# Which engine adds SBUF tiles: GpSimd's share kept for one stretch of a decoder block

## Chip, cores and metric

The kernel runs on one core of one Trainium2 chip, in one launch. Its time is device time in microseconds (us), and lower is better. A core has a matrix engine (TensorE, PE; its weight loads are PEld), VectorE (DVE), ScalarE (ACT), GpSimd (POOL), and a queue (SP) that issues the transfers here. Each engine works off its own queue in order; semaphores tie the queues together. SBUF is the on-chip working memory, and matmuls write to PSUM, which POOL does not read in this kernel.

## What is computed

One decoder block for 1024 tokens of width 1024: a Mamba-2 (SSD) branch and a gated linear attention (GLA) branch from one projection `n @ w_in`, merged by sigmoid gates, then cross-attention to 256 memory tokens, then a SwiGLU FFN of width 2816, with RMSNorm ahead of each and at the end. Cut to its core:

```python
def hybrid_mixer(n, ...):
    z, xBC, dt_raw, q, k, v, r, a1, g_ssd, g_gla = jnp.split(n @ w_in, idx, axis=-1)
    y_ssd = ssd_mixer(z, xBC, dt_raw, ...)
    y_gla = gla_mixer(q, k, v, r, a1, ...)
    merged = sigmoid(g_ssd) * (y_ssd @ w_up_ssd) + sigmoid(g_gla) * (y_gla @ w_up_gla)
    return merged @ w_o

def reference(x, mem, ...):
    h = x
    h = h + hybrid_mixer(rmsnorm(h, norm_mix), ...)
    h = h + mem_cross_attention(rmsnorm(h, norm_xattn), rmsnorm(mem, norm_mem), w_xq, w_xkv, w_xo)
    h = h + swiglu(rmsnorm(h, norm_ffn), w_ffn_in, w_ffn_out)
    return rmsnorm(h, norm_final)
```

## The kernel before

**Products.** A float32 product is made of three products of a narrower float type: each operand x is split into `hi` (a rounded copy, made by ACT) and `lo = x - hi` (a subtraction, on DVE or POOL), and PE adds hi·hi, hi·lo and lo·hi (`split`, line 219). The large projections also use a Strassen-like scheme with seven block products in place of eight. Its sums of blocks are additions of SBUF tiles: those of the activations in `Operands` (lines 226 to 269: operands B11, B21, T1, B22, T2, T3, T4, each with an `h` and an `l` tile), those of the weights in `Unit.left` (lines 290 to 305).

**Units.** A `Unit` makes 256 output columns for all 1024 tokens. It loads `raw` (1 MB of weights), and for each of the seven names it forms the weight block (for T1 the sum `sa` of two blocks; for B22 two subtractions; for T3 one), splits it into `whi` and `wlo`, runs 12 matmuls into an accumulator and evacuates that into `o`. Three accumulators serve a unit: B11, T2, T3 and T4 add up in one of them, T1 and B22 in a second, B21 in a third (line 276), so T4 can't start before T3's result has been read. In PSUM there are four accumulators (`acc`) and four other banks (`bank`).

**Order of the work.** First the memory's k and v and the norm of x, with the operands B formed beside them; then v and two small columns (`v_steps`, line 619, where a weight block is `vraw` and its sum `vsa`); then z (4 units), xBC (6 units, with a convolution), then r, q, k and one gate unit beside the SSD scan; then the other gate units beside the GLA scan; then five dense products (`dense`: w_up_ssd, w_up_gla, w_o, w_xq and, behind the attention, w_xo), with the sums of w_ffn_out's blocks formed beside them (`presum`, line 1190); then the FFN in (22 units, in pairs of gate and up, whose results are multiplied together and stored) and FFN out.

**Who adds.** `DVE` and `POOL` are wrapped in a `Meter` (line 59), which keeps an account `t` of when the engine would be done, by a rate for each. `either` (line 86) gives back the engine that would be done with an addition first; a `slack` of 1 or 2 us in POOL's favour goes with the sums of blocks. `either` is asked by Operands (lines 267 and 268), Unit.left (293, 302), `Stats.take` (465, sums of squares, `ssum`), the split of the memory's weights (561), v_steps (639, 644), the fetch of y's blocks (1175), presum (1200), the merge (1231), the products of gate and up and their block sums (1361 to 1389) and the residual's fold (1498). Other work is put on POOL by name: parts of the convolution and of the SSD scan, small copies, and the power in `rsqrt` (line 207). A plain `DVE` stands for all that reads PSUM, for evacuations above all.

**Queues.** The program is written in an order of its own, and the framework orders each engine's queue when the kernel is built, by priority and by a timeline of its own (line 1606). `ahead()` (line 134) raises the priority of weight blocks and evacuations, and `PRIO` that of the scans' steps. All transfers are issued by SP. As the whole trace shows DVE's and POOL's instructions under line 74 (the Meter's), the groups are told apart by their tiles.

```python
def either(ap, slack=0.0):

    return POOL if POOL.after(ap) - slack < DVE.after(ap) else DVE
```

Of the kernel before, what the change touches and what calls it, by code (L numbers as in the profile page):

```python
# [79 lines left out]
def block_kernel(ctx: ExitStack, tc: tile.TileContext, t: dict, out: bass.AP):  # L80
# [2 lines left out]
    PE, ACT, SP = Tensor(nc.tensor, now), nc.scalar, nc.sync  # L83
    DVE, POOL = Meter(nc.vector, now, 0.06, 1.04e-3), Meter(nc.gpsimd, now, 0.08, 2.25e-3)

    def either(ap, slack=0.0):

        return POOL if POOL.after(ap) - slack < DVE.after(ap) else DVE


    def pool(name, bufs=1, space=None, stack=None, **kw):
# [36 lines left out]
    def bank(dt=F32):  # L128
        return ps.tile([P, 512], dt, name="bank", tag="bank", bufs=4)
# [57 lines left out]
    def col(name, i=0):  # L187
        which, at = gcol[name]
        return cols[:, which, at + i:at + i + 1]
# [199 lines left out]
    def group(units, B, then=(), nxt=None, frm=6, products=7):  # L389


        for u in units:
            u.load()
        then = list(then)
        many = len(units)
        for n, name in enumerate((PAIRED if many > 1 else SPACED)[:products]):
            for x, u in enumerate(units):
                u.step(name, B)
                if many > 1:
                    B.upto((n + 1) * B.kh - (-(x + 1) * B.kh // many))  # L400
                if n == 6 and nxt:
                    nxt.upto((x + 1) * nxt.kh // many)
                if n >= frm and then:
                    then.pop(0).load()
                while len(posts) > lag[0]:
                    settle()
                    if n < 4:
                        break
                yield
        for u in then:  # L410
            u.load()

    def run(main, *rest, prio=0):

        owed = [0.0] * len(rest)
        for _ in main:
            for i, (g, rate) in enumerate(rest):
                owed[i] += rate
                while owed[i] >= 1.0:
                    owed[i] -= 1.0  # L420
                    with tc.high_priority(offset=prio):
                        next(g, None)

    def chain(gs):
        for g in gs:
            yield from g

    def drain(g):
        for _ in g:
            pass  # L430

    def singles(units, B, then=()):

        for u, nxt in zip(units, list(units[1:]) + [None]):
            yield from group([u], B, [nxt] if nxt else then)

    def store_rows(dst, func=None):

        def mk(base):
            def post(i, j, ap):  # L440
                if func is not None:
                    ACT.activation(ap, ap, func)
                SP.dma_start(dst[base + i * P:base + (i + 1) * P, half(j)], ap)
            return post
        return mk

    def w_in_units(c0, n, mk):
        return [Unit(t["w_in"], 0, c0 + 256 * u, post=mk(256 * u)) for u in range(n)]
# [270 lines left out]
    def ssd_prep():  # L719
        bc = lambda r_: r_.unsqueeze(1).to_broadcast([P, NCH, NH])  # L720
        xb, e, l, q = (gp.tile([P, NCH, NH], F32, name=n, tag=n) for n in ("xb", "ex", "ln", "po"))
        m = gp.tile([P, NCH, NH], I32, name="pm", tag="pm")
        add(DVE, xb, dt_t, bc(dtb))
        ACT.activation(e, xb, AF.Abs)
        ACT.activation(e, e, AF.Exp, scale=-1.0)
        ACT.activation(l, e, AF.Ln, bias=1.0)

        DVE.tensor_scalar(q, e, -0.25, 1.0 / 3.0, ALU.mult, ALU.add)
        mul(DVE, q, q, e)
        DVE.tensor_scalar(q, q, -1.0, 0.5, ALU.mult, ALU.add)  # L730
        mul(DVE, q, q, e)
        DVE.tensor_scalar(q, q, -1.0, 1.0, ALU.mult, ALU.add)
        mul(DVE, q, q, e)
        DVE.tensor_scalar(m, e, 0.02, None, ALU.is_lt)
        DVE.copy_predicated(l, m, q)
        DVE.scalar_tensor_tensor(dtv, xb, 0.0, l, ALU.max, ALU.add)
        ea = gp.tile([P, NH], F32, name="ea", tag="ea")
        ACT.activation(ea, alog, AF.Exp)
        a = gp.tile([P, NCH, NH], F32, name="adt", tag="adt")
        DVE.scalar_tensor_tensor(a, dtv, -1.0, bc(ea), ALU.mult, ALU.mult)  # L740
        af = a.rearrange("p c h -> p (c h)")
        yield
        p1, p2, p3 = bank(), bank(), bank()
        PE.matmul(p1[:, :P], triu, af, start=True, stop=True)
        PE.matmul(p2[:, :P], af, triu, start=True, stop=True)
        PE.matmul(p3[:, :P], ones, af, start=True, stop=True)
        ct = gp.tile([P, P], F32, name="ct", tag="ct")
        DVE.tensor_copy(ct, p2[:, :P])
        SP.dma_start(cs_d, ct)
        DVE.tensor_copy(cs, p1[:, :P])  # L750
        sub(DVE, dec, p3[:, :P], cs)
        ACT.activation(dec, dec, AF.Exp)
        ACT.activation(ec, p3[:, :P], AF.Exp)
        yield

    def gla_prep():

        w3, wa2 = (gp.tile([48, 512], d, name=n, tag=n) for n, d in (("w3", F32), ("wa2", F32R)))
        for i in range(3):
            SP.dma_start(w3[16 * i:16 * i + 16], t["gla_w_a2"])  # L760
        ACT.activation(wa2, w3, AF.Copy)
        sub(DVE, wa2[32:48], w3[32:48], wa2[32:48])
        a3 = gp.tile([P, NCH, 48], F32R, name="a3", tag="a3")
        ACT.activation(a3[:, :, 0:16], a1_t, AF.Copy)
        ACT.activation(a3[:, :, 32:48], a1_t, AF.Copy)
        sub(DVE, a3[:, :, 16:32], a1_t, a3[:, :, 0:16])
        idr = gp.tile([P, P], F32R, name="idr", tag="idr")
        ACT.activation(idr, ident, AF.Copy)
        a1T = gp.tile([48, TOK], F32R, name="a1T", tag="a1T")
        keep = gp.tile([P, TOK], F32, name="keep", tag="keep")  # L770
        POOL.memset(keep, 1.0)
        for c in range(NCH):
            POOL.memset(keep[:, c * CH:c * CH + 1], 0.0)
        for j in range(2):
            p = bank()
            for a in range(4):
                PE.matmul(p[:48, a * P:(a + 1) * P], a3[:, 4 * j + a, :], idr, start=True, stop=True)
            DVE.tensor_copy(a1T[:, j * HALF:(j + 1) * HALF], p[:48, :])
        yield
        x_ = gp.tile([P, 4, TOK], F32, name="gx", tag="gx")  # L780
        y_ = gp.tile([P, 4, TOK], F32, name="gy", tag="gy")
        pairs = [slice(h, h + 2) for h in range(0, 4, 2)]
        for h in range(4):
            for j in range(2):
                p = bank()
                PE.matmul(p, wa2[:, h * P:(h + 1) * P], a1T[:, half(j)], start=True, stop=True)
                ACT.activation(x_[:, h, half(j)], p, AF.Identity, bias=col("b_a", h))
            ACT.activation(y_[:, h], x_[:, h], AF.Abs)
            if h % 2:
                yield  # L790
        for h in pairs:
            ACT.activation(y_[:, h], y_[:, h], AF.Exp, scale=-1.0)
            yield
        for h in pairs:
            ACT.activation(y_[:, h], y_[:, h], AF.Ln, bias=1.0)
            yield
        for h in range(4):
            x, y = x_[:, h], y_[:, h]
            DVE.scalar_tensor_tensor(x, x, 0.0, y, ALU.min, ALU.subtract)
            DVE.tensor_tensor_scan(y, keep, x, 0.0, ALU.mult, ALU.add)  # L800
            yv, xv = (v.rearrange("p (c s) -> p c s", s=CH) for v in (y, x))
            bm, bl = yv[:, :, CH // 2 - 1:CH // 2], yv[:, :, CH - 1:CH]
            sub(DVE, xv, yv, bm.to_broadcast([P, NCH, CH]))
            SP.dma_start(bd_d[h * P:(h + 1) * P, :], x)
            POOL.tensor_copy(ebm[:, h], bm.rearrange("p c o -> p (c o)"))
            POOL.tensor_copy(ebl[:, h], bl.rearrange("p c o -> p (c o)"))
            POOL.tensor_copy(ewl[:, h], xv[:, :, CH - 1:CH].rearrange("p c o -> p (c o)"))
            yield
        for e in (ebm, ebl, ewl):
            ACT.activation(e, e, AF.Exp, scale=1.0 / TAU)  # L810
        yield
# [5 lines left out]
    gs = w_in_units(GS0, 4, store_rows(gs_d))  # L817
    gg = w_in_units(GG0, 4, store_rows(gg_d))
    prep = chain([ssd_prep(), gla_prep()])
    run(singles(zu, B, xu[:1]), (prep, .3))  # L820
    drain(prep)
    st2.close()
# [136 lines left out]
    ssd = ssd_steps()  # L959
    run(singles(ru + qk + gs[:1], B, gs[1:2]), (ssd, 16 * 4 / 63), prio=PRIO)  # L960
    drain(ssd)
    st3.close()


# [645 lines left out]
```

## Time and profile before

| | us |
|---|---|
| median of 3 runs | 2016.9 |
| lowest and highest of them | 2014.09 and 2017.74 |
| the profiled execution | 2017.15 |
| its span, from first to last instruction | 2015.4 |

The profile is of that one execution. "Busy" is the time in which an engine has an instruction under way; a group's row gives the line and engine, output tile and inputs, the number of instructions, their busy time and the mean of one, and then the time that the engine sat idle ahead of them and what ended most of it. `<-` in a view of waits reads "waited for". The column PEclk is the share of full speed granted to TensorE. Where a chain of waits is given, it is the work that ended last in that stretch, followed backwards.

The largest groups of POOL's additions over the whole execution, of which the first four are weight sums of units and of presum:

```profile
L74 POOL TENSOR_TENSOR raw<-raw 128x512 f32<-128x512 f32 x68 | 103.6, 1529 | 7.6 <-DVE sa L74 4.8
L74 POOL TENSOR_TENSOR sa<-raw 128x512 f32<-128x512 f32 x56 | 82.6, 1474 | 206.8 <-DMA raw<-in_w_ffn_out_dram 95.2
L74 POOL TENSOR_TENSOR raw<-raw,sa 128x512 f32<-128x512 f32 x48 | 76.8, 1600 | 91.6 <-DVE wlo L74 91.4
L74 POOL TENSOR_TENSOR sa<-sa,raw 128x512 f32<-128x512 f32 x48 | 73.0, 1521 | 172.0 <-DVE wlo L74 172.0
L74 POOL TENSOR_TENSOR o<-o 128x512 f32<-128x512 f32 x39 | 63.4, 1629 | 59.4 <-DVE o L74 34.9
```

### The profile page before, as it was taken

The page shows a single profiled execution, that of the slowest core. Times are in us where ns is not written, and L with a number is a line of the kernel's source. Part 1 is how long each engine was busy: PE and PEld are TensorE (multiplying, and loading weights), DVE is VectorE, ACT ScalarE, POOL GpSimd, SP SyncE. Part 2 cuts the span into 40 slices and gives each one's busy share as a digit, 9 for nine tenths or more (in the row PEclk, how much of TensorE's full clock was granted, in tenths as well). Part 3 has the DMA queues.
Part 4 walks back from the last instruction along what each step waited for, and adds up shares of the span by engine and source line. Part 5 has one row for each costly group of instructions (what it writes and reads, how often), then busy time and mean ns, then how long its engine had stood idle before and what let it go on. Part 6 is the DMA issues. An engine that isn't in the chain of part 4 may idle for free.

```text
span 2015.4 us, 26277 instructions
## 1 busy us (share of the span) xinstructions
PE 1937.9 (96%) x9740; PEld 1617.2 (80%) x9740; DVE 1250.2 (62%) x1763; ACT 897.0 (45%) x1581; POOL 716.9 (36%) x524
## 2 busy tenths in 40 slices
PE   7798899999999999999999999998999999999998
PEld 6797687777777878888878888876888888888887
DVE  5855649879876655633444328566767667674465
ACT  7433844466553555542333226453343343354243
POOL 2612435556554212232134310244454554430002
PEclk9899999999999999999999999999999999999999
DMA  8441332255643755685775520432323323276463
GB/s 286 147 126 62 120 105 106 104 185 184 202 152 115 224 169 157 221 301 193 247 243 188 177 84 22 136 121 89 104 79 110 126 78 105 89 256 228 149 227 127
DMA packets 243365, 309.60 MB, mean 154 GB/s; under 512 B 14986, under 2 KB 162676, under 8 KB 243236
## 3 DMA queue, kind: packets, MB, share of 16 engines
q1 hardware_dynamic: 243236, 307.92, 45.6%
q8 instruction: 76, 1.25, 0.3%
q14 instruction: 53, 0.43, 0.1%
HBM read 211.07 MB, written 96.80 MB: 153 GB/s over the span
## 4 chain that ended last, share of the span: by engine, by line
PE 66%; DVE 8%; DMA 8%; POOL 6%; issue 6%; ACT 4%; SPq 2%; POOLq 0%; ACTq 0%; DVEq 0%
PE acc L52 58%; PE bank L52 7%; POOL raw L74 2%; DVE wlo L74 2%; DVE cv L74 1%; DMA raw<-in_w_in_dram 1%; PE bank L56 1%; POOL sa L74 1%; POOL y L74 1%; ACT whi L220 1%; DVE o L74 1%; DMA sr<-sr_d 1%; DMA vraw<-in_w_in_dram 1%; DMA ga<-yg_d 1%; ACT e L881 1%
## 5 line engine op out<-in xcount | busy, mean ns | idle before, releaser
L52 PE MATMUL acc<-hl,wd 128*128 128x512 f32 x1920 | 439.9, 390 | 1.7 <-DVE hl L74 0.8
L52 PEld LDWEIGHTS acc<-hl,wd 128*128 128x128 f32 x1920 | 360.1, 188 | 77.0 <-DVE hl L74 1.2
L74 DVE TENSOR_TENSOR wlo<-raw,whi 128x512 fp32r<-128x512 f32 x268 | 244.5, 915 | 129.4 <-ACT whi L220 128.7
L220 ACT ACTIVATE whi<-raw 128x512 fp32r<-128x512 f32 x272 | 169.8, 628 | 247.3 <-PE acc L52 194.7
L74 DVE TENSOR_TENSOR o<-acc,o 128x512 f32<-128x512 f32 (+1 forms) x160 | 107.2, 674 | 88.5 <-PE acc L52 85.9
L52 PE MATMUL acc<-fs 128*128 128x512 f32 (+1 forms) x792 | 156.2, 356 | 0.6 <-ACT o L1505 0.5
L74 POOL TENSOR_TENSOR sa<-raw 128x512 f32<-128x512 f32 x56 | 82.6, 1474 | 206.8 <-DMA raw<-in_w_ffn_out_dram 95.2
L52 PEld LDWEIGHTS acc<-fs 128*128 128x128 f32 x792 | 130.7, 189 | 21.6 <-ACT o L1505 0.9
L74 POOL TENSOR_TENSOR sa<-sa,raw 128x512 f32<-128x512 f32 x48 | 73.0, 1521 | 172.0 <-DVE wlo L74 172.0
L220 ACT ACTIVATE fs<-fr 128x1024 fp32r<-128x1024 f32 (+1 forms) x84 | 80.1, 984 | 110.2 <-PE acc L52 43.4
L74 DVE TENSOR_TENSOR fs<-fr,fs 128x1024 fp32r<-128x1024 f32 (+1 forms) x84 | 98.0, 1198 | 39.7 <-ACT fs L220 39.4
L74 POOL TENSOR_TENSOR raw<-raw,sa 128x512 f32<-128x512 f32 x48 | 76.8, 1600 | 91.6 <-DVE wlo L74 91.4
L220 ACT ACTIVATE whi<-sa 128x512 fp32r<-128x512 f32 x96 | 60.4, 629 | 109.2 <-PE acc L52 67.1
L74 POOL TENSOR_TENSOR raw<-raw 128x512 f32<-128x512 f32 x68 | 103.6, 1529 | 7.6 <-DVE sa L74 4.8
L74 DVE TENSOR_TENSOR wlo<-sa,whi 128x512 fp32r<-128x512 f32 x96 | 79.1, 824 | 37.7 <-ACT whi L220 37.5
L74 DVE TENSOR_TENSOR wd<-raw,wd 128x1024 fp32r<-128x1024 f32 x40 | 51.8, 1302 | 65.2 <-ACT wd L220 57.5
L74 DVE TENSOR_TENSOR ga<-acc,ga 128x512 f32<-128x512 f32 x64 | 43.8, 687 | 69.7 <-PE acc L52 56.0
L74 POOL TENSOR_TENSOR o<-o 128x512 f32<-128x512 f32 x39 | 63.4, 1629 | 59.4 <-DVE o L74 34.9
L52 PE MATMUL acc<-B22h,whi 128*128 128x512 f32 x192 | 77.4, 403 | 7.0 <-ACT whi L220 7.0
L52 PE MATMUL acc<-T2h,whi 128*128 128x512 f32 x192 | 77.4, 403 | 3.1 <-ACT whi L220 2.8
L52 PE MATMUL acc<-T2h,wlo 128*128 128x512 f32 x192 | 76.5, 399 | 3.8 <-DVE wlo L74 3.8
L52 PE MATMUL acc<-T1h,whi 128*128 128x512 f32 x192 | 76.2, 397 | 3.8 <-ACT whi L220 3.8
(370 smaller groups left out, 4832.9 us busy)
## 6 DMA issues: line engine op xcount, KB each, us to landing
raw<-in_w_in_dram SPq DMA_DIRECT2D x26, 1024.0 KB, 6.2
raw<-in_w_ffn_in_dram SPq DMA_DIRECT2D x22, 1024.0 KB, 7.6
act_d<-o SPq DMA_DIRECT2D x77, 256.0 KB, 2.0
fr<-act_d SPq DMA_DIRECT2D x35, 512.0 KB, 4.9
raw<-in_w_ffn_out_dram SPq DMA_DIRECT2D x11, 1024.0 KB, 6.9
fr<-down_d SPq DMA_DIRECT2D x20, 512.0 KB, 4.9
down_d<-raw SPq DMA_DIRECT2D x33, 256.0 KB, 2.7
raw<-in_w_xkv_dram SPq DMA_DIRECT2D x8, 1024.0 KB, 10.9
```

Source lines behind the costliest of these rows:

```text
L52: return s.e.matmul(o, x, y, **kw)
L56: return s.e.transpose(o, x, i)
L74: return f(*a, **kw)
L220: ACT.activation(hi, src, AF.Copy)
L881: ACT.activation(s.e[:, h], s.csb[:, h], AF.Relu, bias=cs[:, s.i0 + h:s.i0 + h + 1], scale=-1.0)
```

## The change

`either` gives back POOL only while a flag is set. The flag is set ahead of the first unit behind v (z) and cleared when the SSD scan is done. Outside that stretch every addition that asked `either` goes to DVE, and DVE's account runs on with them. What is put on POOL by name stays there.

```diff
+    shared = [False]
+
     def either(ap, slack=0.0):
 
-        return POOL if POOL.after(ap) - slack < DVE.after(ap) else DVE
+        return POOL if shared[0] and POOL.after(ap) - slack < DVE.after(ap) else DVE
...
     prep = chain([ssd_prep(), gla_prep()])
+    shared[0] = True
     run(singles(zu, B, xu[:1]), (prep, .3))
...
     run(singles(ru + qk + gs[:1], B, gs[1:2]), (ssd, 16 * 4 / 63), prio=PRIO)
     drain(ssd)
+    shared[0] = False
     st3.close()
```

## The prediction

> **What bounds the kernel now.** I began with the profile's page, for its busy shares.
>
> ```profile
> span 2015.4 us, 26277 instructions
> PE 1937.9 (96%) x9740; PEld 1617.2 (80%) x9740; DVE 1250.2 (62%) x1763; ACT 897.0 (45%) x1581; POOL 716.9 (36%) x524
> ```
>
> TensorE (PE) idles 2015.4 - 1937.9 = 77.5 us. Only that, and time in which it ran slowly, can be won. The second view cuts the span into the program's stages (columns: stretch, its length, then busy us and instructions of PE, PEld, DVE, ACT, POOL, then granted clock, DMA share, GB/s).
>
> ```profile
> core 0: us, PE busy (x) PEld busy (x) DVE busy (x) ACT busy (x) POOL busy (x), PEclk, DMA share, GB/s
> 52.00:97.00 45.00, 35.59 (x260) 34.04 (x261) 42.91 (x43) 23.31 (x44) 30.32 (x20) 0.89 0.40 136
> 97.00:175.00 78.00, 77.34 (x635) 77.08 (x636) 40.95 (x77) 25.40 (x45) 11.89 (x14) 1.00 0.34 106
> 175.00:651.00 476.00, 449.46 (x2334) 356.38 (x2333) 359.12 (x515) 255.96 (x471) 236.43 (x177) 0.98 0.42 137
> 651.00:830.00 179.00, 172.48 (x834) 144.74 (x833) 99.98 (x201) 95.24 (x203) 43.30 (x35) 0.99 0.55 172
> 1345.00:1390.00 45.00, 37.20 (x161) 28.06 (x159) 30.40 (x44) 22.74 (x41) 25.42 (x17) 0.96 0.23 76
> 1390.00:1800.00 410.00, 409.82 (x1808) 339.42 (x1809) 292.30 (x336) 166.57 (x281) 203.27 (x133) 1.00 0.33 113
> ```
>
> The stretch from 175 to 651 (the z and xBC units and the SSD scan) keeps the old rule; a third of PE's idle time lies there, out of reach. Elsewhere three stages leave PE idle beside work that the rule places: the start of v (52 to 97, 9.4 us), GLA (651 to 830, 6.5 us) and the start of the FFN (1345 to 1390, 7.8 us). In v's remainder and the FFN's body PE is busy throughout, so nothing can be won there, only lost.
>
> In 52 to 97 VectorE (DVE) is busy 42.91 of 45 us. The view of groups (count, then busy us, mean ns of one, and idle before them) shows that it is slow rather than overloaded; the last row is the same addition later, in 97 to 175, while GpSimd (POOL) does next to nothing.
>
> ```profile
> L74 DVE TENSOR_TENSOR wlo<-raw,whi 128x512 fp32r<-128x512 f32 x10 | 14.5, 1466 | 3.3 <-ACT whi L220 3.3
> L74 DVE TENSOR_TENSOR B22l<-hs,B22h 128x512 fp32r<-128x512 f32 x4 | 5.9, 1497 | 0.0
> L74 DVE TENSOR_TENSOR T1l<-hs,T1h 128x512 fp32r<-128x512 f32 x4 | 4.9, 1228 | 0.0
> L74 DVE TENSOR_TENSOR T2l<-hs,T2h 128x512 fp32r<-128x512 f32 x4 | 4.6, 1200 | 0.0
> L74 DVE TENSOR_TENSOR vraw<-vraw,vsa 128x1056 f32<-128x1056 f32 x1 | 2.3, 2340 | 0.0
> L74 DVE TENSOR_TENSOR wlo<-vraw,whi 128x528 fp32r<-128x528 f32 x2 | 2.0, 1024 | 0.0
> L74 DVE TENSOR_TENSOR T3l<-hs,T3h 128x512 fp32r<-128x512 f32 x4 | 2.5, 688 | 0.0
> ```
>
> The order of time shows why: one kind of addition takes 0.68 or 1.78 us, according to whether POOL is in an addition at that moment.
>
> ```profile
> 58.82 0.68 DVE L74 TENSOR_TENSOR T1l<-hs,T1h 128x512 fp32r<-128x512 f32 x1
> 60.70 1.78 DVE L74 TENSOR_TENSOR T1l<-hs,T1h 128x512 fp32r<-128x512 f32 x1
> 60.24 1.69 POOL L74 TENSOR_TENSOR hs<-hs 128x512 f32<-128x512 f32 x1 [1.89 <-DVE hs L74]
> ```
>
> Where they meet, each takes about 1.7 us, so the pair does two additions in 1.7 us. DVE alone does four in 2.5 us (the row of T3l), so 0.625 us each and 1.25 us for two: both engines together are slower than the faster one alone. The chain of waits and PE's waits say that this stage hangs on DVE:
>
> ```profile
> by line: DVE wlo L74 29.5%; DVE B22l L74 13.0%; DVE T1l L74 10.6%; issue 9.8%; DVE hs L74 8.6%; PE bank L52 7.3%; ACT whi L220 5.4%; DVE vraw L74 5.0%; DVE T2l L74 3.5%; DVE vq L74 2.9%; PE bank L56 1.9%; ACT B22h L220 1.5%; DVE kvs L74 1.3
> PE bank L52 <- DVE wlo L74: 7.0, 4, 3.3
> ```
>
> **The change, part by part.** *Start of v.* POOL gives up these groups:
>
> ```profile
> L74 POOL TENSOR_TENSOR hs<-hs 128x512 f32<-128x512 f32 x14 | 22.0, 1602 | 8.3 <-DVE hs L74 8.3
> L74 POOL TENSOR_TENSOR wlo<-raw,whi 128x512 fp32r<-128x512 f32 x4 | 5.8, 1448 | 12.6 <-ACT whi L220 12.6
> L74 POOL TENSOR_TENSOR vsa<-vsa,vraw 128x1056 f32<-128x1056 f32 x1 | 2.9, 2857 | 3.7 <-DVE wlo L74 3.7
> ```
>
> DVE gains 18 x 0.625 = 11.3 us, and 1.25 us for the one of double width: 12.5 us. It loses the stretching, down to 0.69 us an addition (1.25 for 1056 columns): 10 x 0.78 + 4 x 0.81 + 4 x 0.54 + 4 x 0.51 + 1.1 + 2 x 0.33 = 17.0 us. Net 4.5 us off the engine that sets the end. Bounds: nothing, if PE's next wait is ACT's or a load's; 9.4 us, if every gap closes. I take 4.5, since chain and waits both name DVE. The stage's clock of 0.89 says that some matmuls ran slowly behind the gaps, but what that would give lies behind DVE, so it is not added.
>
> *Start of the FFN.* PE waits here for splits and for the sum of squares; below that, the instructions in front of them in time.
>
> ```profile
> PE acc L52 <- ACT whi L220: 3.1, 4, 1.3
> PE bank L52 <- DVE ssum L74: 2.2, 1, 2.2
> PE acc L52 <- DVE wlo L74: 2.0, 3, 1.5
> 1347.87 4.09 DVE L74 TENSOR_TENSOR T2l<-o,T2h 128x512 fp32r<-128x512 f32 x3
> 1348.03 1.69 POOL L74 TENSOR_TENSOR sa<-sa,raw 128x512 f32<-128x512 f32 x1 [0.63 <-DVE wlo L74]
> 1349.67 1.74 POOL L74 TENSOR_TENSOR o<-o 128x512 f32<-128x512 f32 x1
> 1353.09 2.98 DVE L74 TENSOR_TENSOR T3l<-o,T3h 128x512 fp32r<-128x512 f32 x3
> 1353.84 3.40 POOL L74 TENSOR_TENSOR B22l<-o,B22h 128x512 fp32r<-128x512 f32 x2 [2.42 <-ACT B22h L220]
> 1362.50 3.03 POOL L74 TENSOR_TENSOR sa<-raw 128x512 f32<-128x512 f32 x1 [5.27 <-DMA raw<-in_w_ffn_in_dram]
> ```
>
> Three additions alone take 0.69 + 2 x 0.6 = 1.9 us. So T2l gives back 2.2, T3l 1.1, and the first sum of the up unit, done by DVE in 0.69 us, 2.3: 5.6 us. Four additions of POOL (sa, o, two of B22l) now stand in DVE's queue: 4 x 0.625 = 2.5 us. Net 3.1 us, between 0 and the 7.3 us of the waits. The SP queue is part of it: the second load of FFN weights is issued behind the last store of the residual, which waits for DVE.
>
> *GLA.* PE's waits are mostly ACT's, which loads hold. One is POOL's: `ss` (line 207, which stays on POOL) stood behind a weight sum.
>
> ```profile
> PE bank L56 <- ACT o L1039: 2.7, 2, 2.5
> 722.13 1.27 POOL L74 TENSOR_TENSOR sa<-raw 128x512 f32<-128x512 f32 x1 [8.09 <-DMA raw<-in_w_in_dram]
> 723.36 1.07 POOL L74 TENSOR_TENSOR ss<-ss,mhalf 128x4 f32<-128x4 f32 x1
> ```
>
> With the sum gone, ss starts about 1.2 us earlier and PE behind it too: 1.2 us, between 0 and 2.7.
>
> *FFN body.* All of POOL's 133 additions move: 133 x 0.625 = 83 us. With no stretching undone, DVE would have 292 + 83 = 375 of 410 us; with all of it undone, (336 + 133) x 0.625 = 293 us, as much as now. It fits either way. PE is busy 409.82 of 410, so the gain is nil; a loss is possible (below). The dense products (830 to 1345) and the end of the kernel are taken at nil: PE is busy there but for a few us, and a dense product has four accumulators to wait in, each of 24 matmuls, so 5.4 us at the FFN body's 409.82/1808 = 0.227 us.
>
> Sum: 4.5 + 3.1 + 1.2 = 8.8 us. The profiled execution took 2017.15 us (span 2015.4), 0.25 above the median of 2016.9, so I forecast 2017.15 - 8.8 = 2008.4 us.
>
> **The rivals.** *No net change* (2013 to 2021). The order of each queue is fixed at build with a timeline that this change shifts; the adds may stand in front of what PE waits for, so that the 12.5 us at the start of v come before the wlo that they now sit beside. For it: ACT and loads are already PE's releasers in the FFN's start and in GLA. Against it: DVE's net work falls.
>
> *Slower: DVE waits for weights.* The first sum of a unit needs its weights to have landed. On POOL that wait holds nothing up; in DVE's queue it holds the accumulators' evacuation.
>
> ```profile
> POOL sa L74 <- DMA raw<-in_w_ffn_in_dram: 31.7, 8, 6.0
> 909.06 0.69 DVE L74 TENSOR_TENSOR sa<-raw 128x512 f32<-128x512 f32 x1 [8.70 <-DMA raw<-in_w_ffn_out_dram]
> ```
>
> It has happened: DVE stood 8.70 us in front of one, in the dense products, where the accumulators cover it. In the FFN a product is 12 matmuls of 0.227 us, so 2.7 us, and T3's result must be added before T4 reuses its bank: 2.7 - 0.69 = 2.0 us of cover. From there on it decides. Eight waits of 31.7/8 = 4.0 us cost 8 x 2.0 = 16 us: 2008.4 + 16 = 2024.4. Against it: DVE, with more to do than POOL, comes to these sums later.
>
> *Slower: DVE is simply full.* If the long additions were not POOL's doing, the 12.5 us at the start of v would be added in full to a stage 95% busy: 2017.15 + 12.5 = 2029.7. The alternating 0.68 and 1.78 us speak against it. The Trainium skill, page "Perfetto Trace Analysis", section "Optimizing Scalar/DVE Operations", says that from a saturated DVE it may make sense to move work even to GpSimd, which this change undoes, but warns that the two share a read port, so that it might not help; the trace agrees with the warning (0.68 against 1.78 us).
>
> *The change does less than it says.* Inside the kept stretch the choice could drift, since DVE's account now runs higher. It has little room: the 19 units there already do their four sums on POOL.
>
> ```profile
> L74 POOL TENSOR_TENSOR raw<-raw,sa 128x512 f32<-128x512 f32 x19 | 35.0, 1842 | 60.1 <-DVE wlo L74 60.1
> L74 POOL TENSOR_TENSOR sa<-sa,raw 128x512 f32<-128x512 f32 x19 | 26.2, 1381 | 62.2 <-DVE wlo L74 62.2
> ```
>
> Its time would be that of no change, and its chance is within that one.
>
> **How the numbers follow.** About 0.2% (4 us) is what a measurement of this kernel can tell from no change. Forecast, 2001 to 2012.9: 0.60. No net change: 0.22. DVE waits for weights: 0.13. DVE full: 0.05. So faster 0.60, same 0.22, slower 0.18. The low end adds the upper bounds of the two larger parts (9.4 + 7.3 = 16.7, so 2000.5, taken as 2001). The high end reaches through the case of no change, to 2020.5; what is left out is the two slower cases and a little more, 0.2.
>
> **What would show it.** Right: DVE's additions at 0.69 us in 52 to 97, PE's waits for wlo there under 3 us, that stage some 4 us shorter, PE's idle time from 1345 to 1390 down to about 5, and DVE's busy time in the FFN body near 290 us in spite of 133 more additions. Wrong: DVE idle for a load of weights with PE waiting for DVE's evacuation, in the FFN or GLA; additions still at 1.2 to 1.5 us without POOL; or a shorter start of v whose gain PE loses again before 175 us.

## The result and the profile after

The changed kernel took 2000.46 us (median of 6 runs, 1996.18 to 2004.35) against 2015.66 us for the kernel before (6 runs on the same chip, 2014.09 to 2017.74): ratio 0.9925, 95% interval 0.9911 to 0.994, so some 15.2 us faster. The forecast was 2008.4, and 2000.46 lies just under the low end of its range, 2001.0. From the page of the profile after:

```profile
span 1998.9 us, 26100 instructions
PE 1937.3 (97%) x9740; PEld 1618.6 (81%) x9740; DVE 1303.5 (65%) x2064; ACT 897.9 (45%) x1581; POOL 261.8 (13%) x223
```

PE works as long as before (1937.9 us) and idles 61.6 us instead of 77.5: nearly all of the gain is idle time of PE. POOL has lost 455 us of work, and DVE has taken over 301 additions for 53 us more of busy time. The next view cuts the span where the stages of the prediction begin and end in this execution (columns as there).

```profile
52.00:90.70 38.70, 33.84 (x260) 32.86 (x261) 36.46 (x60) 22.33 (x44) 0.21 (x1) 0.96 0.49 167
167.80:642.00 474.20, 449.37 (x2334) 355.66 (x2333) 357.46 (x516) 255.82 (x471) 234.96 (x179) 0.98 0.42 138
642.00:816.80 174.80, 172.59 (x839) 145.86 (x838) 108.33 (x225) 95.20 (x203) 8.41 (x8) 0.99 0.57 177
1332.60:1375.00 42.40, 37.95 (x161) 29.45 (x159) 31.71 (x59) 22.66 (x41) 3.60 (x2) 0.92 0.26 87
1375.00:1785.00 410.00, 409.84 (x1808) 339.38 (x1809) 302.54 (x468) 166.84 (x281) 0.00 (x0) 1.00 0.34 113
```

The first row holds the same 260 matmuls as 45.00 us before: 6.3 us shorter, with DVE doing 60 instructions in 36.46 us where it did 43 in 42.91 (17 more, not 19: two of the 14 splits `wlo<-raw` now lie behind the end of this stretch). The third row, GLA, has 2.2 us of idle PE (6.5 before) and is 4.2 us shorter. The fourth, the start of the FFN, is 2.6 us shorter. The kept stretch (second row) is 1.8 us shorter, of which more below. In the FFN's body PE is as full as before.

In the start of v, the view of groups shows the additions of DVE at one duration:

```profile
L74 DVE TENSOR_TENSOR hs<-hs 128x512 f32<-128x512 f32 x16 | 10.5, 681 | 0.0
L74 DVE TENSOR_TENSOR wlo<-raw,whi 128x512 fp32r<-128x512 f32 x12 | 8.0, 682 | 2.0 <-ACT whi L222 1.9
L74 DVE TENSOR_TENSOR T1l<-hs,T1h 128x512 fp32r<-128x512 f32 x4 | 2.7, 682 | 0.0
L74 DVE TENSOR_TENSOR B22l<-hs,B22h 128x512 fp32r<-128x512 f32 x4 | 2.6, 680 | 0.0
L74 DVE TENSOR_TENSOR T2l<-hs,T2h 128x512 fp32r<-128x512 f32 x4 | 2.6, 681 | 0.0
```

Before, the same groups had means of 1466 (wlo), 1228, 1497 and 1200 ns. All the stretching is gone, as forecast.

### Stage by stage, over all profiles

One profile of each kernel was taken, and stages in which nothing differs vary between them too. So the table gives the stages of all eleven kernels that have the same tile sizes, in us, each from the first matmul of its first unit to that of the next stage (the GLA column covers six of its seven units; "dense" is the seventh with all that lies between it and the FFN; the last column runs from FFN out's first block sum to the end). The kernels are told in the next section; an asterisk marks a stage in which POOL shares the additions.

| kernel | start to z | z | xBC | SSD | GLA | dense | FFN, first pair | FFN body | FFN out to the end |
|---|---|---|---|---|---|---|---|---|---|
| before | 174.8* | 99.3* | 118.6* | 256.5* | 184.5* | 515.8* | 54.4* | 375.4* | 236.1* |
| after | 167.6 | 97.5* | 118.6* | 256.4* | 179.3 | 517.6 | 51.9 | 375.4 | 234.7 |
| v_only | 167.6 | 98.1* | 118.6* | 254.9* | 184.7* | 517.7* | 54.5* | 375.7* | 236.6* |
| gla_only | 174.3* | 99.2* | 118.6* | 253.3* | 179.9 | 521.4* | 54.4* | 375.4* | 235.7* |
| late_only | 173.8* | 97.7* | 118.6* | 257.4* | 187.5* | 514.0 | 52.9 | 375.4 | 234.7 |
| dve_all | 168.1 | 96.8 | 114.2 | 256.5 | 181.4 | 517.3 | 53.0 | 375.4 | 234.8 |
| scan_only | 166.3 | 96.6 | 116.2 | 256.7* | 180.6 | 517.4 | 52.1 | 375.4 | 234.7 |
| bd2_before | 174.8* | 99.8* | 118.6* | 255.1* | 179.8* | 515.3* | 55.5* | 375.4* | 235.5* |
| bd2_v_only | 169.0 | 98.3* | 118.6* | 253.7* | 179.1* | 513.8* | 54.5* | 375.4* | 235.5* |
| bd2_after | 167.8 | 99.3* | 118.6* | 254.0* | 178.8 | 516.2 | 52.8 | 375.5 | 234.7 |
| bd2_scan_only | 168.9 | 97.9 | 116.3 | 255.5* | 179.8 | 514.2 | 53.3 | 375.4 | 235.1 |

The start and the FFN's first pair fall apart by the rule in that stage alone, with no overlap. GLA does so only among the kernels with one tile for bd. z with POOL sharing runs from 97.5 to 99.8 us, the SSD scan from 253.3 to 257.4 and the dense stretch, under either rule, from 513.8 to 521.4, whatever happens elsewhere; so the 1.8 us that the kept stretch shows between before and after can't be told from chance.

### The profile page after: what moved, and what is told of

Read it like the earlier page. It is cut to its first block, busy times and chain, and to the rows that moved or that the text cites. A ratio compares the mean times of both kernels' runs of the same rounds, so it can differ in the third digit from the quotient of the medians.

```text
span 1998.9 us, 26100 instructions
## 1 busy us (share of the span) xinstructions
PE 1937.3 (97%) x9740; PEld 1618.6 (81%) x9740; DVE 1303.5 (65%) x2064; ACT 897.9 (45%) x1581; POOL 261.8 (13%) x223
## 4 chain that ended last, share of the span: by engine, by line
PE 64%; DMA 11%; DVE 10%; issue 4%; ACT 4%; POOL 4%; SPq 2%; POOLq 0%; ACTq 0%; DVEq 0%
PE acc L52 55%; PE bank L52 8%; DMA raw<-in_w_in_dram 2%; DMA raw<-in_w_ffn_out_dram 2%; DVE cv L74 1%; DVE wlo L74 1%; POOL raw L74 1%; PE bank L56 1%; DMA ga<-yg_d 1%; DMA ysg_d<-ga 1%; POOL y L74 1%; DVE ga L74 1%; DMA ga<-ys_d 1%; DVE o L74 1%; ACT whi L222 1%
## 5 line engine op out<-in xcount | busy, mean ns | idle before, releaser
L74 DVE TENSOR_TENSOR wlo<-raw,whi 128x512 fp32r<-128x512 f32 x272 | 206.3, 761 | 80.8 <-ACT whi L222 80.3
L74 POOL TENSOR_TENSOR rstd<-rstd,mhalf 128x4 f32<-128x4 f32 (+1 forms) x7 | 8.2, 1171 | 1173.4 <-DVE rstd L74 1173.4
L74 DVE TENSOR_TENSOR fs<-fr,fs 128x1024 fp32r<-128x1024 f32 (+1 forms) x84 | 92.5, 1130 | 40.1 <-ACT fs L222 40.0
L74 DVE TENSOR_TENSOR sa<-raw 128x512 f32<-128x512 f32 x40 | 28.0, 700 | 92.7 <-DMA raw<-in_w_ffn_out_dram 46.8
L74 DVE TENSOR_TENSOR wlo<-sa,whi 128x512 fp32r<-128x512 f32 x96 | 67.3, 701 | 31.0 <-ACT whi L222 30.8
L52 PE MATMUL acc<-T1h,wlo 128*128 128x512 f32 x192 | 76.9, 400 | 1.9 <-DVE wlo L74 1.9
L52 PE MATMUL acc<-B21h,whi 128*128 128x512 f32 x192 | 76.4, 398 | 0.6 <-ACT whi L222 0.6
L52 PE MATMUL acc<-T4h,whi 128*128 128x512 f32 x192 | 75.3, 392 | 1.5 <-DVE o L74 1.5
L52 PE MATMUL acc<-T2l,whi 128*128 128x512 f32 x192 | 76.5, 399 | 0.0
L52 PE MATMUL acc<-T3h,whi 128*128 128x512 f32 x192 | 76.2, 397 | 0.3 <-ACT whi L222 0.3
```

The source lines that it names most:

```text
L52: return s.e.matmul(o, x, y, **kw)
L74: return f(*a, **kw)
```

## The experiments

Theory S: the parts of the change gain each for itself, by additions no longer stretched. Its rivals: one part carries it all, or the parts trade with each other.

### The parts alone

Edits are shown against the changed kernel; `...` marks lines left out.

**v_only**: DVE alone only up to z.

```diff
     drain(ssd)
-    shared[0] = False
```

> Only the start (up to the z units) adds on DVE alone; everything behind it chooses between DVE and POOL as the kernel before does. Matched matmuls of the two profiles stand 7.2 us earlier at 175 us and 9.0 us earlier at 651 us in the changed kernel. Theory S (the stages' gains add up, each made in its own stage by additions that no longer meet): 2015.7 - 9.0 = 2006.7 us, between 2005 and 2009. Rival T (the start's gain is a lead that later stages give back unless they are changed too): above 2010 us, with the lead gone by 840 us.

Measured: 2009.61 us (2005.39 to 2018.58), ratio 0.9964, interval 0.995 to 0.9977. The start is 167.6 us, as after the change, and nothing of it is lost by the end. The time lies between the bounds of the two theories and doesn't decide; the stages do, for S.

**gla_only**: DVE alone only from the end of the SSD scan to the end of GLA.

```diff
-    shared = [False]
+    shared = [True]
...
-    shared[0] = True
...
     drain(ssd)
     shared[0] = False
...
     drain(gla)
+    shared[0] = True
```

> Only the stretch from the end of the SSD scan to the end of the GLA scan adds on DVE alone. The profiles' lead grows there from 9.0 to 13.2 us. Theory S: 2015.7 - 4.2 = 2011.5 us, between 2010 and 2013.5. Rival T (what GLA gains comes from the earlier start, since loads and units meet differently): 2014 to 2017 us.

Measured: 2012.25 us (2006.61 to 2017.2), ratio 0.9971, interval 0.9958 to 0.9984. GLA took 179.9 us. S's range holds the time. This part alone brings 4.1 us (2016.33 - 2012.25, the median of the kernel before beside these runs), more than three times the 1.2 us that the prediction gave it.

**late_only**: DVE alone only behind GLA.

```diff
-    shared = [False]
+    shared = [True]
...
-    shared[0] = True
...
-    shared[0] = False
...
     drain(gla)
+    shared[0] = False
```

> Only what lies behind the GLA scan (dense products, attention, FFN) adds on DVE alone. The profiles' lead falls by 0.7 us in the dense products, grows by 2.6 at the FFN's start, by 0 in the FFN's body, and by 1.4 from there to the end. Theory S: 2015.7 - 3.3 = 2012.4 us, between 2011 and 2014. Rival (DVE comes to stand in front of weights that have not landed): above 2016 us.

Measured: 2013.36 us (2008.14 to 2019.17), ratio 0.998, interval 0.9969 to 0.9991, within S's range.

The three ratios fall short of 1 by 0.36, 0.29 and 0.20%, each within some 0.13%, together 0.85%; the whole change by 0.75%, interval 0.60 to 0.89%. So the parts add up, as far as these intervals can tell. That each part's gain is made by additions no longer stretched is the other half of theory S; the next two sections test it.

**dve_all**: the flag is never set, so DVE alone everywhere.

```diff
-    shared[0] = True
     run(singles(zu, B, xu[:1]), (prep, .3))
```

> DVE alone everywhere, the z and xBC units and the SSD scan included: there 77 more additions leave POOL, which keeps the convolution's and the scan's own work. Theory S: additions that meet are slower than DVE alone, there too, so 175 to 651 us gets shorter: 1993 to 1999 us. Rival (in that stretch DVE has no room: 107 us busy of the convolution's 118): that stage gets longer, and the kernel takes 2002 to 2010 us.

Measured: 2000.01 us (1997.21 to 2008.65), ratio 0.9917, interval 0.9898 to 0.9935: between the two expectations, and the same as the change, for all that xBC shows 114.2 us instead of 118.6. Keeping POOL in the stretch up to the end of the SSD scan neither helps nor harms in a way that this run can tell.

**scan_only**: POOL shares in the SSD scan alone.

```diff
-    shared[0] = True
     run(singles(zu, B, xu[:1]), (prep, .3))
...
+    shared[0] = True
     run(singles(ru + qk + gs[:1], B, gs[1:2]), (ssd, 16 * 4 / 63), prio=PRIO)
```

> POOL shares the additions in the SSD scan's stage alone; z and xBC are as with DVE alone. With DVE alone everywhere xBC took 114.2 us against 118.6 with the change, and the kernel was yet no faster (2000.0). If that gain is real and was given back in the SSD scan for want of POOL: 1994.5 to 1998 us, xBC 114 to 115 us, SSD 253 to 257 us. If what xBC gains is only moved (the planner lays the same work later): xBC 114 us, SSD 258 us or more, and the kernel within 1998.5 to 2002 us.

Measured: 1995.99 us (1994.21 to 1999.2, 4 runs), ratio 0.9897, interval 0.987 to 0.9924. The time and SSD (256.7 us) lie within the first forecast; xBC took 116.2 us, above both forecasts, between the 114.2 of dve_all and the 118.6 of the change. It is the fastest placement with one tile for bd, but its interval overlaps with those of dve_all and of the change.

### Is it the meeting of two engines?

Three kernels start from the change and let DVE do every addition, but wherever the old rule would have taken POOL, POOL works beside it on a tile of its own (`idle`), for which nobody waits. A copy of 8 columns of an input ties it to its time; that copy can be waited for, as it reads the input. To make room, `wring` gives tiles of 528 columns instead of 640. No addition is taken off DVE by this.

```diff
     def either(ap, slack=0.0):
-        return POOL if shared[0] and POOL.after(ap) - slack < DVE.after(ap) else DVE
+        if shared[0]:
+            return POOL if POOL.after(ap) - slack < DVE.after(ap) else DVE
+        return Beside if beside[0] and POOL.after(ap) - slack < DVE.after(ap) else DVE
+
+    class Beside:
+        @staticmethod
+        def tensor_tensor(o, a, b, op):
+            r = DVE.tensor_tensor(o, a, b, op)
+            POOL.tensor_copy(idle[:, :8], a[:, :8] if len(a.shape) == 2 else a[:, 0, :8])
+            POOL.tensor_tensor(idle, idle, idle, ALU.mult)
+            return r
...
     def wring():
-        return [wp.tile([P, 640], F32R, name=n, tag=n, bufs=3)[:, :528] for n in ("whi", "wlo")]
+        return [wp.tile([P, 528], F32R, name=n, tag=n, bufs=3) for n in ("whi", "wlo")]
```

**pool_beside_v**: so in the start. **memset_beside_v**: the same, but POOL writes zeros three times in place of the product. **pool_beside_gla**: the first, in GLA instead.

> From the start to z, each addition that the old rule would have given to POOL stays on DVE, and POOL multiplies an idle 128x512 tile of its own beside it, which nobody waits for. Stage from start to z: 174.8 us before, 167.6 after the change. Theory M (what was paid before is that DVE and POOL, working on SBUF at the same moment, both get slower): DVE's additions go from 0.68 us to 1.2 us or more on the mean and the stage goes back to 171 to 178 us, the kernel to 2004 to 2011 us. Rival O (what was paid is POOL as a stop on the way of the limbs, or the order of PE's queue that comes with it): the stage stays at 167 to 168.5 us, the kernel at 1999 to 2002 us.

> As pool_beside_v, but POOL sets its idle tile to zero three times instead of multiplying it: it writes and reads no SBUF operand but the 8 columns that tie it to its time. If theory M holds and it is POOL's reading of two operands that DVE meets: DVE's additions stay at 0.68 to 0.75 us, the stage from start to z at 167 to 169 us, the kernel at 1999 to 2003 us. If any work of POOL on SBUF does it: as pool_beside_v, 171 us or more. Under rival O it stays at 167 to 168.5 us as well, so this run speaks only beside pool_beside_v.

> As pool_beside_v, but in the GLA stage alone; the start is that of the change. GLA stage: 184.5 us before, 179.3 after the change. Theory M: DVE's additions there go from 0.68 us to over 1 us, the evacuations by ACT come late again for PE, and the stage goes back to 182 to 188 us, the kernel to 2003 to 2008 us. Rival O: 178 to 181.5 us, the kernel 1999 to 2002 us.

Measured: 2026.18 us (ratio 1.0054, interval 1.0034 to 1.0073), 2011.22 us (0.9982, 0.9967 to 0.9997) and 2015.03 us (0.9993, 0.9978 to 1.0008). In this order. The whole times miss all expectations, as the three kernels share a loss elsewhere: the FFN's body takes 383.0 to 383.9 us in each, where it was 375.4. They are compared with each other by stage. The start took 182.2 us beside products, 168.7 beside zeros, and 167.9 in pool_beside_gla, where POOL does nothing there. Groups of 52 to 97 us, of pool_beside_v first:

```profile
L74 POOL TENSOR_TENSOR idle<-idle 128x512 f32<-128x512 f32 x15 | 19.5, 1301 | 1.3 <-POOL idle L74 0.2
L74 DVE TENSOR_TENSOR hs<-hs 128x512 f32<-128x512 f32 x16 | 13.9, 890 | 0.0
L74 DVE TENSOR_TENSOR T1l<-hs,T1h 128x512 fp32r<-128x512 f32 x4 | 4.4, 1101 | 0.0
```

And of memset_beside_v, with 11 places of three zeroings each:

```profile
L74 POOL MEMSET idle<- 128x512 f32 x33 | 17.4, 526 | 1.9
L74 DVE TENSOR_TENSOR hs<-hs 128x512 f32<-128x512 f32 x16 | 10.5, 680 | 0.0
```

These are means over additions that meet POOL's work and others that don't (of the four T1l in memset_beside_v, 681 ns on the mean, none does). The order of time shows the meetings themselves. Beside products (pool_beside_v):

```profile
59.91 1.39 POOL L74 TENSOR_TENSOR idle<-idle 128x512 f32<-128x512 f32 x1
60.33 1.52 DVE L74 TENSOR_TENSOR T1l<-hs,T1h 128x512 fp32r<-128x512 f32 x1
62.44 0.68 DVE L74 TENSOR_TENSOR T1l<-hs,T1h 128x512 fp32r<-128x512 f32 x1
```

Beside zeros (memset_beside_v):

```profile
57.01 1.69 POOL L74 MEMSET idle<- 128x512 f32 x3
58.12 0.68 DVE L74 TENSOR_TENSOR hs<-hs 128x512 f32<-128x512 f32 x1
```

Of the 19 additions of 512 columns that a product overlaps in this stretch, the 12 that begin while it runs take 0.89 to 1.52 us; the seven that were under way before it take 0.68, as those that run alone. The 16 additions of 512 columns that a zeroing overlaps all take 0.68 to 0.69 us. So it is POOL's products that meet DVE's additions, and not its zeros; the products read SBUF and the zeros don't. The products cost the start 13.5 us more than the zeros (182.2 against 168.7), of which ACT's two waits for POOL's copies (1.3 and 0.8 us) can explain but a small part. In the start theory M holds: rival O's 167 to 168.5 us is far off. M's own figures were missed, the stage being above its 171 to 178 us and the means (0.89 to 1.10 us) under its 1.2. The 13.5 us are about twice what the change gained in the start; here DVE does all the additions besides.

The lines also say how they meet: the addition of 60.33 ends at 61.85, which is 0.55 us after the product's end at 61.30. The stretched addition of 60.70 that the prediction shows ends 0.55 us after POOL's, too (62.48 and 61.93). Alone, DVE's additions follow each other at 0.6 us. So a stretched one waits for POOL's instruction to end and then does its work in the usual time: the two take turns.

In GLA theory M doesn't hold. The 182.6 us beside products would lie in M's range, but the stage took 183.0 in memset_beside_v and 180.5 in pool_beside_v, whose GLA has no work beside it at all (the change's 179.3 isn't their measure, since matmuls are slower in these three kernels, as the FFN's body shows). And PE's only wait in GLA beside POOL's products (pool_beside_gla, 642 to 825 us) is the one that the changed kernel has too; the stalls that the kernel before shows there (next section) stay away, though DVE's splits are stretched to 0.79 (`wlo<-raw`) and 0.93 us (`wlo<-sa`) on the mean, less than M's "over 1 us":

```profile
PE bank L56 <- ACT o L1058: 3.2, 1, 3.2
```

So another cause was wanted for GLA.

### GLA: the order of ACT's queue and a late load

PE's waits in GLA, in the kernel before (waited for: us in total, times, longest):

```profile
PE acc L52 <- ACT o L355: 3.1, 2, 1.8
PE bank L56 <- ACT o L1039: 2.7, 2, 2.5
```

And after the change:

```profile
PE bank L56 <- ACT o L1043: 2.0, 1, 2.0
```

The first row is gone. It is PE before T3's matmuls, waiting for T2's evacuation. v_only, whose rule in GLA is the old one, shows it in order of time (an excerpt, as the two below: start, us, engine; SPq is the issue of a load; in brackets the idle time before and what ended it):

```profile
717.27 0.68 DVE L74 TENSOR_TENSOR qk<-qk,bd 128x512 f32<-128x512 f32 x1
717.98 0.36 SPq L989 DMA_DIRECT2D bd<-bd_d  x1
720.67 1.28 ACT L998 ACT_TABLE_LOAD   x1 [2.71 <-DMA bd<-bd_d]
721.96 0.63 ACT L998 ACTIVATE e<-bd 128x512 f32<-128x512 f32 x1
722.50 0.58 ACT L357 ACTIVATE o<-acc 128x512 f32<-128x512 f32 x1
723.13 0.50 PE L52 MATMUL acc<-T3h,whi 128*128 128x512 f32 x1 [1.24 <-ACT o L357]
```

`bd` holds a chunk's decays, which ACT turns into exponentials; there is one tile for it. Its next load goes out when DVE's product has read the old one (717.27 + 0.68), and lands near 720.67. ACT stands still for it for 2.71 us, because the exponential of bd is next in its queue; T2's evacuation (L357) stands behind it, and PE waits for that. The kernel after, at the same place:

```profile
716.03 0.61 ACT L355 ACTIVATE o<-acc 128x512 f32<-128x512 f32 x1
717.03 0.62 ACT L357 ACTIVATE o<-acc 128x512 f32<-128x512 f32 x1
719.16 1.28 ACT L999 ACT_TABLE_LOAD   x1 [1.51 <-DMA bd<-bd_d]
720.46 0.64 ACT L999 ACTIVATE e<-bd 128x512 f32<-128x512 f32 x1
```

ACT still waits for bd, but the queue, ordered anew at build, has the evacuation ahead of that wait, and T3 isn't kept. All three kernels with one tile for bd and POOL sharing in GLA show PE's two stalls before T3 (2.7 to 4.5 us together); none of the seven with one tile and DVE alone does, the three with work beside included. Theory Q: this order is GLA's gain, and the additions aren't. Its test leaves POOL's additions and loads bd early:

```diff
-            s.bd = gl.tile([P, 4, CH], F32, name="bd", tag="bd", bufs=1)
+            s.bd = gl.tile([P, 4, CH], F32, name="bd", tag="bd", bufs=2)
```

**bd2_v_only**, **bd2_after**, **bd2_scan_only**, **bd2_before**: that line in v_only, in the change, in scan_only, and in the kernel before.

> v_only (POOL shares the additions in GLA, as before the change) with two tiles for bd instead of one, so that the load of the next chunk's bd needn't wait for the product that reads the old one. In v_only PE stood 1.24 and 1.50 us before T3's first matmul, for ACT's evacuation L357, which stood in ACT's queue behind the exponential of bd (L998), which waited for its load; after the change the evacuation stands ahead of it. Theory Q (GLA's gain is that order of ACT's queue, not the speed of the additions): with the early load ACT doesn't wait at L998, both stalls go, the GLA stage falls from 184.7 us to 180 to 183 us with under 4.5 us of idle PE (6.2 in v_only), the kernel from 2009.6 to 2005 to 2008 us. Rival H (GLA's gain is POOL's additions off the way of the weights and sums): the stage stays at 183.5 to 187 us, the kernel at 2008.5 to 2012 us.

> The changed kernel with two tiles for bd. Theory Q: there is no stall before T3 in it for the early load to take away, so GLA stays at 178 to 182 us and the kernel at 1998 to 2002 us. If the late load costs something else beside the order of ACT's queue: GLA under 177.5 us, the kernel under 1998 us.

> The fastest version so far (POOL shares in the SSD scan alone, 1996.0 us) with two tiles for bd. Theory Q: no stall before T3 to take away, GLA 179 to 182 us, 1994 to 1998 us; if the early load helps in itself, under 1994 us.

> The kernel before the change, POOL sharing everywhere, with two tiles for bd and nothing else. Theory Q (the change gained in GLA only by the order of ACT's queue that came with it, and an early bd load gains the same): GLA 179 to 182 us instead of 184.5, the start as before (174 to 175 us), FFN's first pair as before (54 to 55 us), the kernel 2008 to 2012 us. Rival H (GLA gained by the additions themselves, and what bd2_v_only showed needs DVE alone in the start): GLA 183 us or more, the kernel 2013 us or more.

| kernel | us (runs) | ratio to before | interval | GLA stage | GLA, one bd tile |
|---|---|---|---|---|---|
| bd2_v_only | 2001.72 (6) | 0.9937 | 0.992 to 0.9953 | 179.1 | 184.7 |
| bd2_after | 1998.46 (5) | 0.9913 | 0.9901 to 0.9926 | 178.8 | 179.3 |
| bd2_scan_only | 1995.0 (6) | 0.9895 | 0.9878 to 0.9912 | 179.8 | 180.6 |
| bd2_before | 2011.28 (12) | 0.9972 | 0.9958 to 0.9985 | 179.8 | 184.5 |

In bd2_v_only and bd2_before POOL does its weight sums in GLA as ever, and the stage is as short as after the change. The times and GLA stages of bd2_after, bd2_scan_only and bd2_before lie in theory Q's ranges. ACT's queue in bd2_v_only:

```profile
713.84 1.28 ACT L998 ACT_TABLE_LOAD   x1
715.13 0.63 ACT L998 ACTIVATE e<-bd 128x512 f32<-128x512 f32 x1
716.19 0.58 ACT L355 ACTIVATE o<-acc 128x512 f32<-128x512 f32 x1
717.71 0.58 ACT L357 ACTIVATE o<-acc 128x512 f32<-128x512 f32 x1
```

Here the exponential stands ahead of both evacuations again, but bd has landed, so it doesn't wait. PE loses 0.5 us at T3 instead of 2.7. Theory Q holds; rival H, that POOL's additions lay on the way of the weights, falls in both kernels. bd2_v_only came out faster than expected (2001.72 for 2005 to 2008, GLA 179.1 for 180 to 183): GLA's 5.6 us are not all of the 7.9, and the rest isn't settled; its w_o stage happened to be 3.9 us shorter (87.0 for 90.9, a stage that runs from 87.0 to 93.6 us over the profiles). bd2_scan_only is the fastest kernel here; its interval just touches that of the change, and it hasn't been compared with it directly.

## Why the prediction was wrong in size, point by point

**Start of v** (forecast 4.5 us, bounds 0 to 9.4): right in mechanism, too small. Over the table the start is 174.4 us with POOL (four kernels) and 167.9 without (seven): 6.5 us. In the profile after, the stretch itself is 6.3 us shorter. Of that, 4.55 us are idle time of PE (9.4 before, 4.9 after), as much as the forecast had. DVE's busy time fell by 6.45 us while its idle time stayed at 2.1 to 2.2; some 1.2 us of that are the two splits that now lie behind the stretch, so the net working came to about 5.2, near the 4.5. The other 1.75 us are PE's busy time with the same 260 matmuls, at a granted clock of 0.96 for 0.89: the term that the prediction named and didn't add. Part of that is only moved: before 52 us, with the same 265 matmuls, PE is busy 38.95 us at a clock of 0.97, where it was 37.86 at 1.00. The rest of v behind this stretch gained 0.9 us more, which the sum didn't have either.

**GLA** (forecast 1.2 us, bounds 0 to 2.7): this is the step that failed. It said that `ss` stood behind a weight sum on POOL and that PE would gain what ss gained. In fact PE's wait there (L1039 before) went from 2.7 to 2.0 us only, and it follows no rule: with one tile for bd it is 1.9 to 3.0 us with POOL sharing and 2.0 to 3.0 without. Of v_only, with the old rule in GLA (640 to 820 us):

```profile
PE acc L52 <- ACT o L357: 2.7, 2, 1.5
PE bank L56 <- ACT o L1042: 1.9, 1, 1.9
```

What gained was the wait that the same part set aside in one clause ("mostly ACT's, which loads hold"). The table's kernels with one bd tile take 184.5 to 187.5 us with POOL (three) and 179.3 to 181.4 without (four): 5.3 us on the mean, of which 4.0 are idle time of PE (7.2 against 3.2) and 1.3 its busy time with nearly the same matmuls. That the queues are ordered anew at build stood in the prediction only as a way to lose. In bd2_before and bd2_v_only the idle time is as low (2.6 and 2.4 us), with POOL adding. That this stage gained as much was luck as far as the prediction goes: nothing in it foresaw the new order of ACT's queue.

**Start of the FFN** (forecast 3.1 us, bounds 0 to 7.3): 54.7 us with POOL (five kernels) and 52.7 without (six), so 2.0. The wait for ssum, 2.2 us, has gone; those for ACT's halves of the splits fell from 3.1 to 0.8 us and those for DVE's rose from 2.0 to 3.1; PE's waits in the profile after:

```profile
PE acc L52 <- DVE wlo L74: 3.1, 3, 1.9
PE acc L52 <- ACT whi L222: 0.8, 2, 0.6
```

PE's idle time went from 7.8 to 4.45 us, where "about 5" was forecast. This step was right. What it owes to the stretching and what to the order was not told apart.

**FFN body** (nil): right, 375.4 to 375.7 us under either rule. DVE is busy 302.54 us, near the 293 worked out for additions without stretching and far from the 375 for additions with it.

**End of the kernel** (nil): 235.9 us with POOL, 234.8 without, so 1.1 us gained that the sum didn't have.

**Rival "DVE waits for weights"**: the wait came as described. DVE's waits in the FFN's body after the change:

```profile
DVE sa L74 <- DMA raw<-in_w_ffn_in_dram: 21.2, 9, 3.8
```

Nine waits, 2.4 us on the mean and 3.8 at the longest, against 2.0 us from which a wait was to cost PE time; yet PE idles 0.16 of 410 us. So the price was wrong, and the order of time shows why (an excerpt):

```profile
1432.99 0.58 ACT L355 ACTIVATE o<-acc 128x512 f32<-128x512 f32 x1
1435.99 0.69 DVE L74 TENSOR_TENSOR sa<-raw 128x512 f32<-128x512 f32 x1 [2.18 <-DMA raw<-in_w_ffn_in_dram]
1436.15 0.58 ACT L357 ACTIVATE o<-acc 128x512 f32<-128x512 f32 x1
1438.06 0.69 DVE L74 TENSOR_TENSOR o<-acc,o 128x512 f32<-128x512 f32 x1
1438.31 0.39 PE L52 MATMUL acc<-T3h,whi 128*128 128x512 f32 x1
```

DVE stands while PE is in T2's matmuls and B21's. The accumulators due then, T1's and T2's, are read by ACT (L355, L357); DVE's next one, B21's, comes at 1438.06, 2.1 us after the wait. All nine waits end before B21's last matmul and T3's first. T3's result, on which the price was worked out, isn't due there. **Rival "DVE is full"**: fell with the 0.68 us of every addition.

**The sum.** 6.5 + 5.3 + 2.0 + 1.1 = 14.9 us, where 15.2 were measured (interval 12.1 to 17.9) and 8.8 forecast. That these agree to 0.3 us is partly chance: between the two profiles z gained 1.8 us and the dense stretch lost 1.8, and neither is in the sum. Of the 6.1 us that the forecast's sum lacked, 4.1 are GLA's. Another 1.5 us of the distance between forecast and result are its starting point, the profiled run's 2017.15 us, where the median is 2015.66. The range's low end took the upper bounds of the start and of the FFN, but not those of GLA, whose own bound was too tight as well.

## What to carry to other kernels

Before an addition is given to a second engine, compare the first one's duration with and without that engine at work beside it, and whether one's end sets the other's: two engines that took 1.7 us for two additions were worth less than one that took 0.68 for each. Where the framework orders the queues anew at build, look behind every in-order wait for a load, and ask who stands behind it; such a wait can cost or gain as much as the edit itself, and a second tile for the load (one word here, 0.28% by itself) takes the wait away under either order. A bound on a stage should be the stage's idle time, not the one wait that the edit is meant to touch.

## What was not expected of the hardware

POOL's zeros, 526 ns each and 17.4 us of them in 45, left DVE's additions at 0.68 to 0.69 us, while its products stretched those that began beside them to as much as 1.52. The Trainium skill, page "Perfetto Trace Analysis", section "Optimizing Scalar/DVE Operations", speaks of a read port that the two engines share; that writing alone doesn't disturb agrees with it.

POOL can wait for DVE far longer than the other way round. In memset_beside_v a copy of 32 columns, which takes 0.2 us in the profile after, took 11.09 us, while DVE added without a pause. It ended 0.1 us after the start of the first of DVE's instructions in that time that reads PSUM:

```profile
73.47 11.09 POOL L74 COPY dt_t<-vq 128x32 f32<-128x32 f32 x1
84.42 0.68 DVE L74 TENSOR_TENSOR kvs<-bank,mbc 128x512 f32<-128x512 f32 x1
```

Another copy, of 8 columns, took 5.54 us from 64.21 and ended in the same way, at DVE's next reading of PSUM (69.62). So what stays on POOL can be held up by a DVE that is given all the additions. That reading of the two lines was not tested by a run of its own.

In the three kernels with work beside, the weight tiles were cut from 640 to 528 columns, with the same part of them in use, and a tile `idle` was added. The FFN's body took at least 383.0 us instead of 375.4, at a granted clock of 1.00 and with PE busy throughout. From the profile after and then from memset_beside_v, the same 380 us (columns as in the view by stages):

```profile
1395.00:1775.00 380.00, 380.00 (x1678) 314.65 (x1677) 281.48 (x436) 157.39 (x264) 0.00 (x0) 1.00 0.33 110
```

```profile
1395.00:1775.00 380.00, 380.00 (x1644) 308.74 (x1643) 273.84 (x428) 150.45 (x259) 0.00 (x0) 1.00 0.31 102
```

That is one matmul every 226.5 ns against every 231.1, so 2.1% slower, which is the whole loss. The two edits were not tried apart. Whether it is where the tiles lie that matters to PE is a guess that no run here tests.
